# Row broadcasts in a three-block kernel: from a diagonal and a product to transposes of a repeated column

## The chip, the cores and the metric

The kernel runs on one core of one Trainium2 chip. The metric is the device time of an execution in microseconds; of each kernel several runs are taken and their median is compared. Profiles are of one execution each, with times from the start of its span.

## The reference

Three residual blocks follow each other, on 1024 tokens of 1024 features, all in float32. Cut to what the change touches:

```python
def rmsnorm(x, g):                      # before every block part, on branches, at the end
    return x * rsqrt(mean(x * x, -1) + EPS) * g

def first_block(x, mem, ...):
    h = rmsnorm(x, norm_g)
    x_m, o_m, z_m, q_d, k_d, v_d, z_d, q_c, z_c = split(h @ w_in)
    y_m = mlstm(...)                    # below, 4 heads, chunks of 128 tokens
    y_d = rmsnorm(diff_attention(q_d, k_d, v_d), dnorm_g) * silu(z_d)   # per head
    y_c = attention over rmsnorm(mem, mem_norm_g) * silu(z_c)
    return rmsnorm(x + concat(y_m, y_d, y_c) @ w_out, final_g)

def mlstm step(C, n, m; q, k, v, i, b):     # one chunk of one head, b = cumsum(log f)
    m_t = maximum(b + m, max_s(d)),  d[t, s] = b[t] - b[s] + i[s]  for s <= t
    s_qk = (q k^T) * exp(d - m_t)           # the row m_t over all keys
    h = (s_qk v + exp(b + m - m_t) C q) / maximum(|den|, exp(-m_t))
```

Block 2 is chunked attention and spatial gating, then a gated feed-forward; block 3 is a gated recurrence and a long convolution, each with an RMS norm of its branch, then a squared-ReLU feed-forward. Each begins and ends with RMS norms like the one above.

## The kernel before

Activations lie with features on the partitions and tokens on the free axis, in two halves of 512 tokens. Large products split both operands into a high and a low part (`split`, L151 and L152) and take three matmuls each (`mm3`, L142 to L144), in units of eight times three matmuls of 512 columns. Weights come through `wraw` and are split by L76 (ScalarE) and L77 (VectorE).

A norm over features is a sum over partitions, so its scale comes out by tokens. `norm_gen` makes it for one half: the squares are summed in `acc` (at the seams between blocks by GpSimd, L183), `sums_to_cols` (L191) turns the sums into columns `ps[:, t]` with one token per partition, L285 and `rsqrt` (L167 to L172, eleven small VectorE instructions) give the scales `nr`, and `bcast_cols` must spread them: every partition needs the row of all 512 scales. It multiplies the identity by the scales into `diag` (L198, VectorE), and a product of an all-ones matrix with `diag` (L202) puts the row on every partition of a PSUM tile `tp`. ScalarE copies it to `rbc` (L298), and eight `nt` tiles (L301) with their splits are the normed tokens that the next products read.

`bcast_cols` is called 30 times: in `norm_gen` for the five norms at the seams and the two spilled ones (14), once for the memory (256 columns), eight times for the heads of the differential attention (`diff_end`), four times for the branches of block 3 (`branch_norm`), and three times at the end (`final_gen`, pieces of 512, 256 and 256 tokens). A seam does the last products of a block by halves, so the norm of the first half runs beside the products of the second.

The mLSTM is `mlstm_gen` and, per head, `mlstm_head`. Its maxima are rows of a tile `nM`: 32 partitions (head, chunk), 128 tokens each. For four chunks at a time the head computes scores (L808, `k` and `q`) into one half of a PSUM tile and the row of `nM` that belongs to the chunk, on all partitions, into the other (L809: a repeated column of the identity with 32 partitions, times `nM`). VectorE, ScalarE and VectorE make `dm` of both (L813 to L816), and products follow with L825, L840 and L850. Four heads with two such groups make eight blocks.

The work is written as generators: the large products yield after every twelve matmuls, and at each yield every side generator (norms, heads) goes one step. A scheduler then sets the order on each engine by priorities and by its own estimate of when operands are ready; ends of products go ahead by `PRIO_E`. Each engine takes its instructions in that order. Small temporaries, `diag` and `nt` among them, share the pool `half` with four buffers; `tp` has two.

Of the kernel before, what the change touches and what calls it, by code (L numbers as in the profile page):

```python
# [8 lines left out]
F32 = mybir.dt.float32  # L9
# [11 lines left out]
# the ends of products go ahead of other instructions on their engines, by so many  # L21
PRIO_E = 300
# units of products between the end of a half and its norm, by the norm's gain
LEAD = dict(norm_g=1, norm_mix_2=3, norm_ffn_2=3, norm_mix_g_3=3, norm_mlp_g_3=3)
LEAD_F = 2
FINAL = (0, 512), (512, 256), (768, 256)   # pieces of the tokens in the last products
FF_GROUPS = (2, 4, 4, 4, 4, 4)
# units of weights that go ahead on the first half of the tokens after a norm
LAG = 3
LAG_3 = 4  # L30
# products into block 3: values and gates of the long convolution, inputs and gates of the recurrence
SEQ_3 = ["v0 g0 x0 v1 g1 x1 v2", "g2 x2 v3 g3 x3 l0 l1 l2 l3"]   # the convolution of a pair after each
UNITS_3 = [(c[0], int(c[1])) for q in SEQ_3 for c in q.split()]

# ---------------------------------------------------------------- column vectors, one column per 128 features
# [16 lines left out]
class Weights:  # L52
    """The packed weight units in the order of their use: loaded ahead, split into high and low parts."""
# [35 lines left out]
class Kern:  # L89
# [8 lines left out]
    # ------------------------------------------------------------ driver  # L98
# [15 lines left out]
    # ------------------------------------------------------------ tiles  # L114
# [21 lines left out]
    # ------------------------------------------------------------ pieces  # L136
    def mm3(self, ps, w, woff, wn, x, xoff, xn, first, last):
        """ps += w^T x with both operands in two parts; w: [128, 2, .], x: [128, 2, .]."""
# [7 lines left out]
    def split(self, dst, off, n, src, scale=None):  # L146
        """dst[:, 0/1, off:off+n] = high and low part of src (* scale)."""
# [9 lines left out]
    def split2(self, dst, off, n, src):  # L157
        """the same into two tiles"""
        hi, lo = (d[:, off:off + n] for d in dst)
        self.nc.scalar.copy(hi, src)  # L160
        self.nc.vector.tensor_sub(lo, src, hi.bitcast(F32))

    def rsqrt(self, y, v, n, parts=128):
        """y = 1/sqrt(v) for small [parts, n] tiles."""
# [9 lines left out]
    def square_sum(self, acc, src, first, scale=1.0, eng=None):  # L174
        """acc (+)= (src * scale)^2"""
# [12 lines left out]
    def sums_to_cols(self, ps, off, acc, n):  # L188
        """ps[:, off+t] = sum over partitions of acc[:, 128 t + partition]"""
# [4 lines left out]
    def bcast_cols(self, cols, n):  # L194
        """[128, n*128] psum: every partition holds the row whose columns are cols[:, :n]"""
        nc = self.nc
        d = self.half_tmp("diag")
        nc.vector.tensor_tensor(d[:, :n * 128].rearrange("p (t c) -> p t c", t=n),  # L198
# [1752 lines left out]
```

## Time and profile before

| | |
|---|---|
| runs, us | 3480.6, 3486.04, 3488.21 |
| median, us | 3486.04 |
| span of the profiled execution, us | 3484.2 |
| TensorE busy | 3385.5 us, 97% |
| VectorE busy | 1750.7 us, 50% |
| ScalarE busy | 1054.5 us, 30% |
| GpSimd busy | 248.0 us, 7% |
| chain that ended last | TensorE 85%, VectorE 8%, issue 4%, ScalarE 2%, DMA 1% |

A busy TensorE is not one at its peak: matmuls overlap, and a record runs from its start to its modelled end. How long an instruction holds the engine is read from start to start in the view of instructions in order of time. Idle time before an instruction counts only where the engine is the one that sets the end.

### The profile page before, as it was taken

To read this page: it belongs to the slowest core of one execution; us is meant where nothing else is said; L and a number is where in the kernel's file an instruction comes from. 1 tells how busy PE (TensorE), PEld (TensorE's weight loads), DVE (VectorE), ACT (ScalarE), POOL (GpSimd) and SP (SyncE) were. 2 spreads that over 40 slices of the span, in tenths; PEclk is the share of its full clock that TensorE was granted. 3 is DMA by queue.
4 is the path that set the end of the run, shared out by engine and by line. 5 is a ranking of instruction groups with operands and counts; after the bars stand their busy time and mean duration, and the time that the engine had idled before them with its cause. 6 is when DMAs were issued, how large, how long until landed. Compare 5 with 4: busy or idle time off the path is not lost.

```text
span 3484.2 us, 41001 instructions
## 1 busy us (share of the span) xinstructions
PE 3385.5 (97%) x16424; PEld 2750.6 (79%) x16424; DVE 1750.7 (50%) x3329; ACT 1054.5 (30%) x1853; POOL 248.0 (7%) x239
## 2 busy tenths in 40 slices
PE   7999999999999999999999999999999999999998
PEld 6787877777778888887788888877877788888887
DVE  7455556664755561546432333354569833333334
ACT  4222244433444532213111111144443421111112
POOL 0000000002100000102000000040211200000002
PEclk9999999999999999999999999999999999999999
DMA  5123211312111243421111111122111111111111
GB/s 182 62 95 117 79 61 43 110 67 85 61 45 45 73 162 142 148 85 44 61 49 49 49 49 49 49 85 62 45 49 73 37 55 49 49 49 49 49 49 55
DMA packets 98383, 245.06 MB, mean 70 GB/s; under 512 B 12944, under 2 KB 31504, under 8 KB 98192
## 3 DMA queue, kind: packets, MB, share of 16 engines
q1 hardware_dynamic: 84816, 199.92, 16.6%
q0 software_dynamic: 11360, 39.80, 3.3%
q8 instruction: 129, 2.11, 0.2%
q10 hardware_dynamic: 2016, 2.72, 0.2%
q14 instruction: 62, 0.51, 0.0%
HBM read 196.20 MB, written 46.20 MB: 70 GB/s over the span
## 4 chain that ended last, share of the span: by engine, by line
PE 85%; DVE 8%; issue 4%; ACT 2%; DMA 1%; POOL 0%; POOLq 0%; SPq 0%; DVEq 0%; ACTq 0%
PE mm L142 24%; PE mm L143 24%; PE mm L144 24%; PE mm L1614 1%; DVE sp L152 1%; PE tp L202 1%; DVE wsplit L77 1%; DVE nt L301 1%; PE tp L142 1%; PE tp L143 1%; PE sc L934 1%; PE sc L1213 1%; PE tp L1232 1%; PE tp L191 1%; PE tp L144 1%
## 5 line engine op out<-in xcount | busy, mean ns | idle before, releaser
L142 PE MATMUL mm<-sp,wsplit 128*128 128x512 f32 x3424 | 1366.7, 400 | 9.4 <-DVE g L1024 3.9
L143 PE MATMUL mm<-sp,wsplit 128*128 128x512 f32 x3424 | 1349.1, 394 | 12.0 <-DVE sp L152 11.1
L144 PE MATMUL mm<-sp,wsplit 128*128 128x512 f32 x3424 | 1350.3, 395 | 0.0
L142 PEld LDWEIGHTS mm<-sp,wsplit 128*128 128x128 f32 x3424 | 648.1, 189 | 155.4 <-issue 9.8
L143 PEld LDWEIGHTS mm<-sp,wsplit 128*128 128x128 f32 x3424 | 649.4, 190 | 144.0 <-DVE sp L152 14.2
L144 PEld LDWEIGHTS mm<-sp,wsplit 128*128 128x128 f32 x3424 | 648.5, 189 | 137.5 <-issue 3.5
L76 ACT CAST wsplit<-wraw 128x1024 fp32r<-128x1024 f32 x264 | 276.7, 1048 | 675.4 <-PE mm L144 629.6
L77 DVE TENSOR_TENSOR wsplit<-wraw,wsplit 128x1024 fp32r<-128x1024 f32 x264 | 325.7, 1234 | 177.2 <-ACT wsplit L76 175.7
L183 POOL TENSOR_TENSOR acc<-acc,sqt 128x512 f32<-128x512 f32 (+1 forms) x105 | 139.7, 1342 | 1525.7 <-ACT sqt L182 1437.1
L142 PE MATMUL mm<-hid,wsplit 128*128 128x512 f32 (+1 forms) x544 | 207.3, 381 | 0.0
L143 PE MATMUL mm<-hid,wsplit 128*128 128x512 f32 (+1 forms) x544 | 207.1, 381 | 0.0
L144 PE MATMUL mm<-hid,wsplit 128*128 128x512 f32 (+1 forms) x544 | 206.3, 379 | 0.0
L1480 DVE TENSOR_TENSOR u<-u,mm 128x512 f32<-128x512 f32 x144 | 98.9, 687 | 185.3 <-PE mm L144 185.2
L1117 DVE SCALAR_TENSOR_TENSOR u<-mm,u 128x512 f32<-128x512 f32 x128 | 88.0, 690 | 170.0 <-PE mm L144 170.0
L1498 DVE TENSOR_TENSOR hd<-hd 128x512 f32<-128x512 f32 x64 | 44.3, 692 | 190.5 <-ACT hd L1497 190.5
L142 PEld LDWEIGHTS mm<-hid,wsplit 128*128 128x128 f32 x544 | 102.2, 188 | 21.5 <-issue 0.2
L143 PEld LDWEIGHTS mm<-hid,wsplit 128*128 128x128 f32 x544 | 102.5, 188 | 20.9 <-issue 0.2
L144 PEld LDWEIGHTS mm<-hid,wsplit 128*128 128x128 f32 x544 | 102.2, 188 | 20.2
L384 DVE SCALAR_TENSOR_TENSOR silu<-silu,mm 128x512 f32<-128x512 f32 x44 | 30.2, 687 | 165.9 <-ACT silu L383 165.9
L1497 ACT ACTIVATE hd<-mm 128x512 f32<-128x512 f32 x64 | 38.2, 598 | 219.1 <-PE mm L144 219.1
L1163 DVE TENSOR_TENSOR silu<-silu,mm 128x512 f32<-128x512 f32 x44 | 30.2, 687 | 126.8 <-PE mm L144 126.8
L383 ACT ACTIVATE silu<-mm 128x512 f32<-128x512 f32 x44 | 26.3, 598 | 184.1 <-PE mm L144 184.1
(511 smaller groups left out, 3792.7 us busy)
## 6 DMA issues: line engine op xcount, KB each, us to landing
wraw<-W SPq DMA_DIRECT2D x264, 512.0 KB, 3.2
x_d<-u SPq DMA_DIRECT2D x32, 256.0 KB, 2.0
t_d<-gl SPq DMA_DIRECT2D x32, 256.0 KB, 2.0
u<-x_d POOLq DMA_DIRECT2D x16, 512.0 KB, 6.3
gl<-t_d POOLq DMA_DIRECT2D x32, 256.0 KB, 3.1
x<-xT SPq DMA_DIRECT2D x16, 256.0 KB, 5.4
u<-xT POOLq DMA_DIRECT2D x8, 512.0 KB, 6.0
bias<-bias POOLq DMA_DIRECT2D x4, 640.0 KB, 4.2
```

What stands on the lines that cost most here:

```text
L76: K.nc.scalar.copy(s[:, 0, :], r)
L77: K.nc.vector.tensor_sub(s[:, 1, :], r, s[:, 0, :].bitcast(F32))
L142: t.matmul(ps, wh, xh, start=first, stop=False)
L143: t.matmul(ps, wh, xl, start=False, stop=False)
L144: t.matmul(ps, wl, xh, start=False, stop=last)
L152: nc.vector.tensor_sub(lo, src, hi.bitcast(F32))
L183: eng.tensor_add(acc, acc, t[:, :acc.shape[-1]])
L191: self.nc.tensor.matmul(ps[:, off + t:off + t + 1], acc[:, t * 128:(t + 1) * 128], self.ones[:, 0:1], start=True, stop=True)
L1117: nc.vector.scalar_tensor_tensor(uu(m, h), ps, 0.5, uu(m, h), op0=OP.mult, op1=OP.add)
L1480: nc.vector.tensor_add(uu(m, h), uu(m, h), ps)
L1497: nc.scalar.activation(t, ps, AF.Relu)
L1498: nc.vector.tensor_mul(t, t, t)
```

## The change

`bcast_cols` no longer builds a diagonal. For each of its columns it calls a new function `row_of`, which transposes the column, read 128 times over, with the identity: four transposes of 128 columns (two in the narrow calls) take the place of one VectorE instruction and one product. The mLSTM uses the same function: `nM` is transposed once in the preparation into 32 more columns of `mcols`, and each row product L809 becomes a transpose of one such column. Comments are dropped as well; line numbers after L196 move by one or two.

```diff
     def bcast_cols(self, cols, n):
-        nc = self.nc
-        d = self.half_tmp("diag")
-        nc.vector.tensor_tensor(d[:, :n * 128].rearrange("p (t c) -> p t c", t=n),
-                                self.ident[:, None, :].to_broadcast([128, n, 128]),
-                                cols[:, :n, None].to_broadcast([128, n, 128]), op=OP.mult)
         ps = self.tp()
-        nc.tensor.matmul(ps[:, :n * 128], self.ones, d[:, :n * 128], start=True, stop=True)
+        for t in range(n):
+            self.row_of(ps[:, t * 128:t * 128 + 128], cols[:, t:t + 1])
         return ps
...
+    def row_of(self, out, col):
+        self.nc.tensor.transpose(out, col.to_broadcast([128, 128]), self.ident)
...
         nc.tensor.matmul(ps[:, 128:160], self.ones[:32, :], d[:32, :32], start=True, stop=True)
-        cols = self.small([128, 160], F32, "mcols", 1)
-        nc.vector.tensor_copy(cols, ps[:, :160])
+        nc.tensor.transpose(ps[:, 160:192], nM, self.ident[:32, :32])
+        cols = self.small([128, 192], F32, "mcols", 1)
+        nc.vector.tensor_copy(cols, ps[:, :192])
...
                 nc.tensor.matmul(ps[:, c * 128:c * 128 + 128], k[:, s], q[:, s], start=True, stop=True)
-                nc.tensor.matmul(ps[:, 512 + c * 128:640 + c * 128],
-                                 self.ident[:32, r0 + c:r0 + c + 1].to_broadcast([32, 128]), nM, start=True, stop=True)
+                self.row_of(ps[:, 512 + c * 128:640 + c * 128], cols[:, 160 + r0 + c:161 + r0 + c])
```

The order on the engines follows. A row is line, operation, output tile, its operands (the moving one first) and size; the new transposes carry L203. On TensorE, the end of the first mLSTM block before (scores, row, then the first products of a branch):

```order
L808 MATMUL sc<-mq,mk 128x128
L809 MATMUL sc<-rw,ident 128x128
L142 MATMUL mm<-sp,wsplit 128x512
L143 MATMUL mm<-sp,wsplit 128x512
L144 MATMUL mm<-sp,wsplit 128x512
```

and now, where the scores have moved to L809:

```order
L809 MATMUL sc<-mq,mk 128x128
L203 MATMUL sc<-ident,mcols 128x128
L142 MATMUL mm<-sp,wsplit 128x512
L143 MATMUL mm<-sp,wsplit 128x512
L144 MATMUL mm<-sp,wsplit 128x512
```

The order is the same; the row product is now a transpose. On TensorE, at the norm of the second half of the tokens ahead of block 1 (`nr` are its scales), the difference:

```order
-L142 MATMUL mm<-sp,wsplit 128x512
-L143 MATMUL mm<-sp,wsplit 128x512
-L144 MATMUL mm<-sp,wsplit 128x512
-L142 MATMUL mm<-sp,wsplit 128x512
-L202 MATMUL tp<-diag,ones 128x512
+L203 MATMUL tp<-ident,nr 128x128 x4
+L142 MATMUL mm<-sp,wsplit 128x512
+L143 MATMUL mm<-sp,wsplit 128x512
+L144 MATMUL mm<-sp,wsplit 128x512
+L142 MATMUL mm<-sp,wsplit 128x512
```

Four products that stood ahead of the broadcast stand behind it. The same is found at nearly every norm: nine products at both halves of the seams ahead of blocks 2 and 3 but one (three there), seven at the first halves of the two other seams, two to six elsewhere. On VectorE, at the first seam, first half, behind the last step of the reciprocal square root before:

```order
L172 SCALAR_TENSOR_TENSOR nr<-rsq_t,nr 128x8
L77 TENSOR_TENSOR wsplit<-wraw,wsplit 128x1024
L198 TENSOR_TENSOR diag<-ident,nr 128x512
L557 TENSOR_TENSOR u_5896<-u_5896,mm 128x512
L301 SCALAR_TENSOR_TENSOR nt<-u_5888,ngg,rbc 128x512
```

and now:

```order
L172 SCALAR_TENSOR_TENSOR nr<-rsq_t,nr 128x8
L77 TENSOR_TENSOR wsplit<-wraw,wsplit 128x1024
L301 SCALAR_TENSOR_TENSOR nt<-u_5894,ngg,rbc 128x512
L557 TENSOR_TENSOR u_5902<-u_5902,mm 128x512
L301 SCALAR_TENSOR_TENSOR nt<-u_5896,ngg,rbc 128x512
```

The diagonal is gone from between the scales and the first normed tile (the numbers behind `u` are names of the eight tiles of the residual, and are counted otherwise in the two programs).

## Rows read from the trace of the kernel before

**Rows 1.** The page: busy time and share by engine; granted clock in 40 slices.

```profile
PE 3385.5 (97%) x16424; PEld 2750.6 (79%) x16424; DVE 1750.7 (50%) x3329; ACT 1054.5 (30%) x1853; POOL 248.0 (7%) x239
...
PEclk9999999999999999999999999999999999999999
```

**Rows 2.** Groups by line and shape, TensorE: busy us, mean ns | idle before.

```profile
L1232 PE MATMUL tp<-ident,p 128*128 128x128 f32 x240 | 39.1, 277 | 2.6 <-DVE p L1223 0.8 <-DVE pt L152 0.7 <-DVE sp L152 0.7
...
L202 PE MATMUL tp<-diag,ones 128*128 128x512 f32 x54 | 34.7, 732 | 18.6 <-DVE diag L198 18.2
...
L202 PE MATMUL tp<-diag,ones 128*128 128x256 f32 x6 | 3.1, 619 | 10.1 <-DVE diag L198 10.1
```

**Rows 3.** TensorE in order of time, dense broadcast: start us, us, line.

```profile
2773.15 1.02 PE L202 MATMUL tp<-diag,ones 128*128 128x512 f32 x2
...
2774.24 0.40 PE L142 MATMUL mm<-sp,wsplit 128*128 128x512 f32 x1
2774.47 0.39 PE L143 MATMUL mm<-sp,wsplit 128*128 128x512 f32 x1
```

**Rows 4.** The same view: four transposes among products.

```profile
614.15 0.60 PE L542 MATMUL tp<-ident,vt 128*128 128x128 f32 x4
...
614.81 0.39 PE L143 MATMUL mm<-sp,wsplit 128*128 128x512 f32 x1
```

**Rows 5.** The same view: broadcasts at half clock, idle time in brackets.

```profile
832.20 3.75 PE L202 MATMUL tp<-diag,ones 128*128 128x512 f32 x4 [2.72 <-DVE diag L198]
...
2619.70 2.08 PE L202 MATMUL tp<-diag,ones 128*128 128x512 f32 x2 [3.61 <-DVE diag L198]
```

**Rows 6.** Views of lines L809 and L808: count, ns min/median/max, first and last start.

```profile
L809 PEld LDWEIGHTS sc<-rw,ident x64: 180/182/184, 179.1 to 360.8; 32*128 32x128 f32 x64
...
L808 PEld LDWEIGHTS sc<-mq,mk x64: 186/188/192, 178.7 to 360.4; 128*128 128x128 f32 x64
```

**Rows 7.** TensorE in order of time: the first mLSTM block, start and end.

```profile
178.80 0.38 PE L808 MATMUL sc<-mq,mk 128*128 128x128 f32 x2
...
182.02 0.76 PE L142 MATMUL mm<-sp,wsplit 128*128 128x512 f32 x1
```

**Rows 8.** The same view: sixteen records on 128 partitions.

```profile
174.13 1.95 PE L789 MATMUL sc<-mw,xm 128*128 128x128 f32 x16
175.84 0.36 PE L142 MATMUL mm<-wsplit,sp 128*128 128x256 f32 x1
```

**Rows 9.** Busy time by stretch, sum of seven stretches from 76 to 420 us.

```profile
sum 344.00, PE 343.04 PEld 272.97 DVE 183.32 ACT 89.11 POOL 3.75; mean PE 49.01 PEld 39.00 DVE 26.19 ACT 12.73 POOL 0.54
```

**Rows 10.** View of line L198: count, ns min/median/max.

```profile
L198 DVE TENSOR_TENSOR diag<-ident,nr x17: 426/691/1769, 38.0 to 3476.1; 128x512 f32<-128x512 f32 x15, 128x256 f32<-128x256 f32 x2
```

**Rows 11.** Chain that ended last, first seam: start us, us, what.

```profile
872.92 1.76 DVE diag L198
```

**Rows 12.** TensorE in order of time, first seam.

```profile
892.68 0.80 PE L143 MATMUL mm<-sp,wsplit 128*128 128x512 f32 x1 [2.71 <-DVE sp L152]
```

**Rows 13.** Chain that ended last, at the end of the program.

```profile
3476.14 0.44 DVE diag L198
...
3476.63 1.24 PE tp L202 x2
```

**Rows 14.** Busy time of L809 by stretch: us, PE (x), PEld (x), clock, DMA.

```profile
178.67:182.08 3.41, 1.92 (x8) 1.17 (x8) 1.00 0.30 92
...
342.51:345.92 3.41, 1.91 (x8) 1.14 (x8) 1.00 0.20 77
```

**Rows 15.** By stretch: us, PE, PEld, DVE, ACT, POOL busy (x), clock, DMA.

```profile
182.08:185.49 3.41, 3.41 (x9) 2.71 (x9) 1.82 (x5) 0.63 (x1) 0.00 (x0) 0.50 0.74 254
...
345.92:349.33 3.41, 3.41 (x9) 2.67 (x9) 1.40 (x4) 0.63 (x1) 0.00 (x0) 0.50 0.47 159
898.88:1612.20 713.32, 704.99 (x3695) 580.84 (x3693) 369.98 (x818) 256.53 (x547) 51.45 (x72) 1.00 0.27 92
```

More of the change, by code (lines that the diff above doesn't have):

```diff
@@ L740, in mlstm_gen @@
         nc.tensor.matmul(ps[:, 128:160], self.ones[:32, :], d[:32, :32], start=True, stop=True)
-        cols = self.small([128, 160], F32, "mcols", 1)
-        nc.vector.tensor_copy(cols, ps[:, :160])
+        nc.tensor.transpose(ps[:, 160:192], nM, self.ident[:32, :32])
+        cols = self.small([128, 192], F32, "mcols", 1)
+        nc.vector.tensor_copy(cols, ps[:, :192])
         yield
-        self.mctx = (xcv, xm, cols, nM)
+        self.mctx = (xcv, xm, cols)
         for h in range(4):
@@ L763, in mlstm_head @@
         nc, v, A = self.nc, self.v, self.A
-        xcv, xm, cols, nM = self.mctx
+        xcv, xm, cols = self.mctx
         ks = 128 ** -0.5
```

## Prediction

> **What bounds the kernel now.** Read the page first: TensorE is busy 97% of the span, VectorE 50%, and the granted TensorE clock is near full in every slice [rows 1]. So TensorE's own work is the bound, and VectorE matters only where TensorE stands and waits for it. Three questions follow: how long does TensorE hold for the work that the change replaces, how long does it wait for the diagonals, and at which clock does it run there. The grouped view answers the second: before the products of the row broadcasts TensorE sat idle 18.2 + 10.1 = 28.3 us for the diagonal of L198 [rows 2]. That is the whole wait, of which the diagonal is only the last link; the sums, the scaling and the reciprocal square root stand before it and stay.
>
> **Term A: the broadcast's product, 30 calls.** 27 calls have 512 columns and 3 have 256; the 54 and 6 records of [rows 2] are two passes for each. In a dense stretch the pair starts at 2773.15 and the second product behind it at 2774.24, 1.09 us later, with one ordinary product (0.23 us from start to start) in between: 0.86 us of TensorE [rows 3]. The new form is four transposes of 128 columns. Four transposes of a value tile start at 614.15 and the second product behind them at 614.81: 0.66 - 0.23 = 0.43 us [rows 4]. So a wide call saves 0.43 us and a narrow one half of it: 27 x 0.43 + 3 x 0.215 = 12.3 us. Five calls ran at half clock, where both forms cost double: the two that start at 832.20 take 3.75 us together, the last of the five, at 2619.70, takes 2.08 [rows 5]. Each is worth another 0.43 us: 2 us.
>
> The stationary operand of the new transposes is one column read 128 times. The row products of the mLSTM have such an operand already, a repeated column of the identity, and its load takes 182 ns, no more than the 188 ns of a full tile [rows 6]. So I charge nothing for the repetition.
>
> **Term B: the rows of the mLSTM, 8 blocks.** Each block has four score products (L808) and four row products (L809, 32 partitions) in turn, two records each. The first holds TensorE from 178.80 to 182.02, 3.22 us [rows 7]; the seven others are built alike. Sixteen records of the same kind as L808's, all on 128 partitions (L789), start at 174.13, and the next product at 175.84 [rows 8]: 1.71 us, with what the next one loses about 1.8, or 0.11 each. In the block a record holds TensorE for 0.2 us; the alternation between 128 and 32 partitions is the only difference that the rows show. The change removes it: the row comes from a transpose over 128 partitions. Eight score records at 0.11 and four transposes at 0.11 make 1.33 us. Saved: 1.89 x 8 = 15.1 us. In the stretches from 76 to 420 us, which hold the mLSTM, TensorE is busy for 343 of 344 us and VectorE for 183 [rows 9], so this is gained in full: the products of the output gates and branches fill the time. The dm chain behind the block keeps the same twelve products ahead of L840 as its cover. If a record of the new block holds 0.2 us like one of the old, the block is 12 x 0.2 = 2.4 us or a little more and B is about 6. I take 15.1, as the rows of L789 are the nearer ones; 6 stays as the lower end. The one new transpose in the preparation (0.11 us) and the copy that is 32 columns wider are counted as nothing, since dense products surround them.
>
> **Term C: waits.** The diagonal takes 0.69 us in the median and 0.43 at 256 columns, but up to 1.77 [rows 10]; 1.75 or more are those at the first and third seam, while GpSimd adds squares. Taking it away shortens a wait by no more than its time and a handover of 0.06. TensorE stood idle before 16 of the 30 calls: three long diagonals at 1.81, six at 0.75, three narrow ones at 0.49 and four waits that were shorter than the diagonal (0.86 together) give 12.2 us at most. Where the norm holds up TensorE to its end, all of that counts: at the first seam the chain is diagonal (872.92, 1.76 us), product, scaled tokens [rows 11], and TensorE waits again, 2.71 us, for the last split of that chain at 892.68 [rows 12]. So it is at the third seam (two waits), at the second and fourth, at 832, in the norm of the memory and at the very end, where 0.44 us of diagonal and a product of 1.24 us follow each other [rows 13]. These make 3 x 1.8 + 3 x 0.75 + 2 x 0.5 = 8.7, and the shorter last product some 0.5 more than A has counted: 9 us.
>
> Against that stands the order: the scheduler now puts the transposes up to nine products earlier. TensorE takes its work in order, so products that used to run ahead of the broadcast and cover the reciprocal square root now stand behind it. Where the norm is not waited for later (second halves of the seams, branch norms, the last pieces, the differential heads), some 50 small and large products are moved, by 0.23 us for a large one [rows 3] about 11 us; the diagonals there and the slack that the old order had give some 7 back. So I take 4 us off: C = 9 - 4 = 5. Its ends are -7 (the moved products cost more than their diagonals save, the seams give nothing) and 12. The second broadcast at the seams that spill a norm needs no wait of its own any more, as its scales are ready with the first; that is within these ends.
>
> **Term D: the clock.** Three stretches of the mLSTM ran at half clock, 182.08 to 185.49 the first and 345.92 to 349.33 the last [rows 15]. What TensorE did before each was such a block: the 3.41 us ahead of it hold all eight row records of one [rows 14]. The other five blocks were followed by none. A block of 1.33 us leaves dense products in the rest of such a stretch, so I expect the three to go: 3.41 us at half clock loses 1.7 us, three times, 5.1 us. Ends 0 and 10, if a low stretch at a seam goes as well.
>
> **Off the path:** 30 diagonals, some 20 us of VectorE's time, and the buffers of the `half` pool that they held. VectorE is not the bound; at the seams this is inside C. VectorE gets no new work but the 32 columns.
>
> **Sum.** A 12.3 + 2, B 15.1, C 5, D 5.1: 39.5 us off the profiled span of 3484.2 gives 3444.7. The median of the runs, 3486.04, lies 1.9 us above that span, so 3447 us.
>
> **Rivals.**
> *The block keeps its cost* (B at 6, D at 0): 12.3 + 2 + 6 + 5 = 25 us, 3461. For it: L808's records, on 128 partitions themselves, hold 0.2 us in the block too [rows 7], so the turn from one kind of product to another may be what costs. Against: products behind transposes start without such a delay [rows 4]. Chance 0.14.
> *The order takes the waits back* (C at -7): 27.5 us, 3459. For it: the order shows the shift at nearly every norm. Against: the starved seams are limited by the chain and not by where the broadcast stands. Chance 0.15.
> *More goes than that* (C at 12, D at 10): 51.4 us, 3435. Chance 0.05.
> *The clock falls behind transposes, slower than before.* If a group of transposes is idleness to the clock, each of the 30 calls and 8 blocks is followed by a stretch like that of [rows 15], 1.7 us lost: 38 x 1.7 = 65 us, against 34 us gained without D. That gives 3517; it decides from about 20 of the 38 places on. The trace speaks against it: 240 transposes of L1232 [rows 2] lie in the attention of block 2, and from 898.88 to 1612.20 the clock was 1.00 [rows 15]. Chance 0.03. The Trainium skill says just this of the clock (TensorE: Matmul & The Clock Gate, Part 4: PE-mode transpose): a transpose does not count as work for the clock, and the full rate does not engage on it. By that rule the time would be this rival's; the trace does not bear it out for groups of two to four transposes among products.
> *It doesn't do what it says*: the repeated column loads slowly. At four times the 0.11 us the 38 groups would take 1.3 us more each, 49 us, and the gain of 39.5 would turn to a loss of 10, 3496. Against: the load of 182 ns [rows 6]. Chance 0.03.
> The forecast keeps 0.60.
>
> **Range and chances.** About 0.2% (7 us) is what a measurement of this kernel can tell from no change. The forecast's own spread is some 9 us, from the places where half-clock stretches happen to fall. Down to 3434 the range takes in the case of more, up to 3465 the two cases of less; the slower rivals and the tails, about 0.16, stay outside. Faster: the forecast, both cases of less and that of more, 0.94, less a little for tails: 0.92. Same 0.03, slower 0.05.
>
> **What would show it.** Right: four transposes hold TensorE 0.43 us in a dense stretch; the mLSTM block lasts 1.3 us, and no half clock follows it; the idle time before the broadcasts stays near 28 us, now against the reciprocal square root, while the waits for the splits at the seams shrink by 1 to 2 us. Wrong: a block of over 2 us; idle time before the transposes well over 30 us with the waits at the seams unchanged; half-clock stretches in dense parts that had none; weights (L77) that come later because VectorE's order has changed.

## The result, and the profile after

The changed kernel took 3446.97 us in the median (3442.71 to 3449.89), the kernel before 3483.32 (3477.88 to 3488.21): a ratio of 0.9894, with a 95% interval of 0.988 to 0.9908. Faster by 36 us. The forecast was 3447, which was 39 us below the 3486.04 that the kernel before had then. Two repeats beside the experiments below gave 3450.03 and 3450.85 us, ratios 0.9911 and 0.9914, or 30 to 32 us. The time lies in the forecast's range; of the four terms, the mLSTM's held, and the others need the account at the end.

The page of the profiled execution (span 3441.0 us): busy time by engine, and the chain that ended last by engine.

```profile
PE 3343.3 (97%) x16447; PEld 2730.7 (79%) x16447; DVE 1732.3 (50%) x3299; ACT 1054.0 (31%) x1853; POOL 249.8 (7%) x239
...
PE 82%; DVE 8%; issue 7%; ACT 2%; DMA 1%; POOL 0%; POOLq 0%; DVEq 0%; SPq 0%; ACTq 0%
```

Against [rows 1], TensorE is busy for 42 us less and the span is 43 us shorter. What is left, TensorE's idle time, was 98.7 us and is 97.7: the change took work off TensorE (and time at half clock, which counts as busy), and in sum it took off hardly any waiting. That is the first thing to read here, since term C had 5 us for waits.

TensorE in order of time, a broadcast in a dense stretch, beside [rows 3]: start us, us, line, shapes.

```profile
2730.90 0.60 PE L203 MATMUL tp<-ident,nr 128*128 128x128 f32 x4
2731.25 0.48 PE L142 MATMUL mm<-sp,wsplit 128*128 128x512 f32 x1
2731.57 0.39 PE L143 MATMUL mm<-sp,wsplit 128*128 128x512 f32 x1
```

From 2730.90 to the second product behind, less one product of 0.23: 0.44 us, where 0.86 stood. And the first mLSTM block, beside [rows 7]:

```profile
175.88 0.39 PE L809 MATMUL sc<-mq,mk 128*128 128x128 f32 x2
176.11 0.27 PE L203 MATMUL sc<-ident,mcols 128*128 128x128 f32 x1
...
177.10 0.27 PE L203 MATMUL sc<-ident,mcols 128*128 128x128 f32 x1
177.13 0.48 PE L142 MATMUL mm<-sp,wsplit 128*128 128x512 f32 x1
```

Twelve records, 0.11 us from one start to the next, 1.25 us to the next product and about 1.33 with what that product loses; the block of before held 3.22. All eight are alike (1.24 or 1.25 us). The loads of the repeated column (count, ns min/median/max, first and last start) cost no more than those of full tiles in [rows 6]:

```profile
L203 PEld LDWEIGHTS tp<-ident,nr x64: 132/136/227, 36.5 to 3433.9; 128*128 128x128 f32 x64
L203 PEld LDWEIGHTS sc<-ident,mcols x32: 137/139/139, 176.0 to 337.3; 128*128 128x128 f32 x32
```

The part of the program with the blocks lies between the first transpose of the gates (L700) and the last transpose of the heads (L878). Those two lines, of the kernel before and then of the changed one:

```profile
L700 PE MATMUL tp<-ident,gt x1: 270/270/270, 145.6 to 145.6; 128*32 128x128 f32 x1
L878 PE MATMUL tp<-ident,ht x32: 270/327/330, 215.0 to 380.1; 128*128 128x128 f32 x32
```

```profile
L700 PE MATMUL tp<-ident,gt x1: 270/270/270, 142.6 to 142.6; 128*32 128x128 f32 x1
L878 PE MATMUL tp<-ident,ht x32: 270/327/332, 206.5 to 356.4; 128*128 128x128 f32 x32
```

234.5 us became 213.8. By stretch (length, then busy time and count by engine, granted clock, DMA), the changed kernel has full clock there (granted 1.00, the level of 2.4 GHz), and over most of what follows; the second line is one of its stretches at half clock (0.50, 1.2 GHz):

```profile
76.00:398.00 322.00, 321.05 (x1757) 260.11 (x1756) 181.15 (x511) 88.98 (x144) 3.76 (x7) 1.00 0.28 94
807.56:817.80 10.24, 7.30 (x20) 5.37 (x21) 5.89 (x12) 3.60 (x6) 1.73 (x3) 0.50 0.22 64
872.41:2319.66 1447.25, 1429.62 (x6906) 1179.31 (x6906) 642.15 (x1186) 407.31 (x756) 89.67 (x102) 1.00 0.21 73
```

None of the three half-clock stretches of [rows 15] is left. The Trainium skill (TensorE: Matmul & The Clock Gate, Part 4: PE-mode transpose) holds that a transpose does not count for the clock; here the 32 transposes of the blocks stand in the first stretch and the clock stays at 1.00, so groups of this size among products do not bring it down. Whether a transpose alone would keep it up, no run here shows.

Last, the idle time of TensorE just before the broadcasts (busy us, mean ns | idle before, by what ended it):

```profile
L203 PE MATMUL tp<-ident,nr 128*128 128x128 f32 x64 | 10.2, 280 | 7.7 <-DVE nr L172 7.6
```

Together with 5.9 us before the two transposes of the memory's norm, 2.5 before the heads' and 2.5 before the branch norms' it is 18.6 us, where [rows 2] had 28.7 (28.3 of it for the diagonal). It fell by 10 us, and yet the sum of all idle time stayed nearly the same: the waiting went elsewhere. The forecast had said the opposite, that these 28 us would stay and other waits shrink.

### The profile page after: what moved, and what is told of

It is laid out like the page before. It is cut to its first block, busy times and chain, and to the rows that moved or that the text cites. A ratio compares the mean times of both kernels' runs of the same rounds, so it can differ in the third digit from the quotient of the medians.

```text
span 3441.0 us, 41019 instructions
## 1 busy us (share of the span) xinstructions
PE 3343.3 (97%) x16447; PEld 2730.7 (79%) x16447; DVE 1732.3 (50%) x3299; ACT 1054.0 (31%) x1853; POOL 249.8 (7%) x239
## 4 chain that ended last, share of the span: by engine, by line
PE 82%; DVE 8%; issue 7%; ACT 2%; DMA 1%; POOL 0%; POOLq 0%; DVEq 0%; SPq 0%; ACTq 0%
PE mm L142 24%; PE mm L143 24%; PE mm L144 23%; DVE sp L152 1%; PE mm L1614 1%; DVE nt L301 1%; DVE wsplit L77 1%; PE sc L1213 1%; PE tp L1232 1%; PE tp L142 1%; PE tp L143 1%; PE tp L191 1%; PE tp L144 1%; PE sc L934 1%; DVE wsplit L1596 0%
## 5 line engine op out<-in xcount | busy, mean ns | idle before, releaser
L142 PE MATMUL mm<-sp,wsplit 128*128 128x512 f32 x3424 | 1362.0, 398 | 15.7 <-DVE u L1117 4.1
```

Of the source, the lines that this page charges most:

```text
L142: t.matmul(ps, wh, xh, start=first, stop=False)
```

## Experiments

Each theory is told with its run. The first question is which half of the change gives what; the second, what the alternation of 128 and 32 partitions and what the diagonal itself had cost; the third, what half clock is worth. A fourth came up on the way.

**The changed kernel again.** No edit.

> The changed kernel once more, five rounds, so that the others of this call have it beside them. If what differs between its executions is the clock alone, its times and granted clocks go together: a mean clock lower by 0.001 is about 6.9 us more at half clock and so at most 3.4 us more time. Expected 3442 to 3450 us with clocks of 0.993 to 0.991.

3450.03 us (3448.99 to 3452.46), ratio 0.9911 [0.9897, 0.9924].

> The changed kernel as it is, as the control for the three kernels beside it: 3447 to 3451 us where the kernel before takes 3482, ratio .990 to .991. Between its profiled executions the mean granted clock should again decide: .991 goes with a span of about 3448 us, .993 with about 3441.

3450.85 us (3448.97 to 3454.06), ratio 0.9914 [0.99, 0.9927]. The profiled spans were 3447.8 and 3448.8, that of the first profile 3441.0. Part of the difference is half clock in the differential attention, between the first transpose of its values and the last of its probabilities: 6.8 us in the first profile, 17.1 and 27.3 in these, 3.4 before. The stage is 2.9 and 6.6 us longer than in the first profile. In the first repeat the start of the program, up to the gates, took another 3.0 us more, and in both the second seam 1.6. Two such stretches of the third profile, by length, busy time and count of TensorE, its loads, VectorE, ScalarE and GpSimd, granted clock, DMA:

```profile
671.64:681.88 10.24, 10.12 (x27) 6.25 (x27) 7.06 (x17) 5.02 (x13) 0.13 (x1) 0.50 0.44 176
750.15:760.39 10.24, 10.24 (x21) 5.99 (x21) 4.89 (x9) 2.15 (x5) 0.00 (x0) 0.50 0.01 2
```

**The broadcasts alone.** The mLSTM is as before (the diff is cut to its row products):

```diff
-                self.row_of(ps[:, 512 + c * 128:640 + c * 128], cols[:, 160 + r0 + c:161 + r0 + c])
+                nc.tensor.matmul(ps[:, 512 + c * 128:640 + c * 128],
+                                 self.ident[:32, r0 + c:r0 + c + 1].to_broadcast([32, 128]), nM, start=True, stop=True)
```

> Only the 30 broadcasts are changed; the mLSTM rows are made as before, by L809-like products on 32 partitions. By the prediction's terms A and C: 12 + 2 + 5 = 19 us faster than before, about 3464. If the idle time is only moved (C = 0), 12 to 14 us, about 3470. If the broadcasts bring only clock, and TensorE's saved work is lost at the seams, under 9 us. In both, the mLSTM blocks still take 3.2 us each and two to four of them are followed by half clock.

3467.39 us (3466.68 to 3472.34), ratio 0.9963 [0.995, 0.9975]: 14.3 us gained. The forecast for this half was 14.3 of work (A) and 5 of waits (C). Half clock behind blocks of the old form is there again, though only twice in this execution, and the part with the blocks took 233.0 us instead of 234.5: the third stretch had cost about half its length.

```profile
236.44:239.86 3.42, 3.42 (x9) 2.65 (x9) 1.70 (x5) 0.63 (x1) 0.00 (x0) 0.50 0.49 153
359.32:362.74 3.42, 3.42 (x10) 2.64 (x9) 1.35 (x4) 0.63 (x1) 0.00 (x0) 0.50 0.00 0
```

**The mLSTM alone.** The broadcasts are as before (the diff is cut):

```diff
-        for t in range(n):
-            self.row_of(ps[:, t * 128:t * 128 + 128], cols[:, t:t + 1])
+        d = self.half_tmp("diag")
+        nc.vector.tensor_tensor(d[:, :n * 128].rearrange("p (t c) -> p t c", t=n),
+                                self.ident[:, None, :].to_broadcast([128, n, 128]),
+                                cols[:, :n, None].to_broadcast([128, n, 128]), op=OP.mult)
+        nc.tensor.matmul(ps[:, :n * 128], self.ones, d[:, :n * 128], start=True, stop=True)
```

> The changed mLSTM alone (row_of for the scores, the norms' broadcasts by diagonal and ones as before). Theory (the two halves of the change do not touch each other): the kernel with the broadcasts alone was 14.3 us faster than before, the whole change 31.7, so this one gains 17 us, or 20.7 by the stage from the mLSTM's gates to its end (234.5 to 213.8 us); no half clock in that stage. Rival (the halves share waits on VectorE, so the gain of one depends on the other): less than 14 us or more than 24 us.

3463.71 us (3460.48 to 3466.82), ratio 0.9948 [0.9936, 0.9961]: 17.5 us gained. With the other half 31.8, and the whole gained 30.4 and 31.7 in the two repeats: the halves add up, as the theory had it. Inside, the mLSTM part took 213.8 us here as in the whole change, 20.7 less than before. That the run gained only 17.5 has a likely place a stage later: the differential attention had 10.2 us at half clock, where the profiles of the kernels with the old blocks had 3.4 to 6.8, and from the third head's sums to the fourth's it took 89.8 us instead of 86.6. These are single executions, so it is a reading and no proof.

**The row as an ordinary product.** The same operands and the same place, but no transpose: two records for each row, 128 partitions.

```diff
-        self.nc.tensor.transpose(out, col.to_broadcast([128, 128]), self.ident)
+        self.nc.tensor.matmul(out, col.to_broadcast([128, 128]), self.ident, start=True, stop=True)
```

> As the changed kernel, but row_of is an ordinary product of the same two operands (repeated column, identity) and no transpose: two passes in place of one, still on 128 partitions, still without a diagonal. A wide broadcast then holds TensorE 8 x 0.11 = 0.88 us again, 12 us in all, and an mLSTM block 16 x 0.11 = 1.8 us, 3.6 us in all: 3460 to 3465. That is if the old block was long because it alternated between 128 and 32 partitions. If it was long because products and row products alternated at all, the blocks stay near 3 us and the half clock behind them comes back: 3475 to 3482.

3458.79 us (3457.11 to 3461.31), ratio 0.9938 [0.9924, 0.9951], 8.8 us above the changed kernel beside it. That is less than the 15.6 us which the expectation had for the additional records. Its profile ran 42.0 us at half clock, that of the changed kernel beside it 61.5; half of the difference is 9.8 us and would explain what is missing, but no run shows that the two belong together. TensorE in order of time, start and end of its first block:

```profile
177.82 0.39 PE L809 MATMUL sc<-mq,mk 128*128 128x128 f32 x2
178.04 0.39 PE L203 MATMUL sc<-ident,mcols 128*128 128x128 f32 x2
...
179.38 0.39 PE L203 MATMUL sc<-ident,mcols 128*128 128x128 f32 x2
179.53 0.47 PE L142 MATMUL mm<-sp,wsplit 128*128 128x512 f32 x1
```

Sixteen records, as many as in [rows 7], in 1.71 us instead of 3.22, and the part took 217.2 us with no half clock. So 1.5 of the 1.9 us a block had nothing to do with transposing: two kinds of product in turn cost nothing, products on 128 and on 32 partitions in turn cost nearly twice their time. This settles the rival in which the block keeps its cost. The four records fewer are the rest.

This run changed the operands together with the partitions, so look at where the time went in the old block. Its loads of stationary operands, kernel before, in order of time:

```profile
178.68 0.31 PEld L808 LDWEIGHTS sc<-mq,mk 128*128 128x128 f32 x2
179.11 0.29 PEld L809 LDWEIGHTS sc<-rw,ident 32*128 32x128 f32 x2
179.52 0.30 PEld L808 LDWEIGHTS sc<-mq,mk 128*128 128x128 f32 x2
```

Two loads on the same number of partitions overlap and start 0.11 us apart. At a change of the number the next load starts only 0.12 us after the last has ended, about 0.3 us from start to start. It is so at all 64 changes in the eight blocks, in both directions, and 8 x 0.19 us is the 1.5 us of a block. With the ordinary product, loads of two kinds on 128 partitions start 0.11 us apart throughout. Elsewhere in the kernel before, from products on 48 partitions (L1399) to products on 16 (L1400), the loads are 0.21 us apart at all twelve changes and 0.11 within a pair.

**The repeated columns written out by VectorE.** All else is as changed; the transposes read a tile of 512 columns that VectorE has to fill first, so the chain has its old length and the products their new one.

```diff
+        d = self.half_tmp("diag")
+        self.nc.vector.tensor_tensor(d[:, :n * 128].rearrange("p (t c) -> p t c", t=n),
+                                     self.ones[:, None, :].to_broadcast([128, n, 128]),
+                                     cols[:, :n, None].to_broadcast([128, n, 128]), op=OP.mult)
         for t in range(n):
-            self.row_of(ps[:, t * 128:t * 128 + 128], cols[:, t:t + 1])
+            self.nc.tensor.transpose(ps[:, t * 128:t * 128 + 128], d[:, t * 128:t * 128 + 128], self.ident)
```

> As the changed kernel, but VectorE writes the repeated columns of a broadcast into a tile of 512 columns (one instruction of 0.69 us, in the place and of the size of the old diagonal), and the transposes read that tile. TensorE's work is that of the changed kernel, VectorE's chain that of before. Term C as predicted (the diagonal was worth time on the chains of the seams): 5 us slower than the changed kernel, up to 9. If VectorE's part was worth nothing, since the idle time of TensorE is as long without it: within 2 us of the changed kernel.

3454.94 us (3451.13 to 3455.62), ratio 0.9921 [0.9908, 0.9935], 4.9 us above the changed kernel by the medians, with intervals that overlap.

**The diagonal built, and read by no one.** VectorE has its old work, behind the transposes; the chain to the transposes is the new one.

```diff
         for t in range(n):
             self.row_of(ps[:, t * 128:t * 128 + 128], cols[:, t:t + 1])
+        d = self.half_tmp("diag")
+        self.nc.vector.tensor_tensor(d[:, :n * 128].rearrange("p (t c) -> p t c", t=n),
+                                     self.ident[:, None, :].to_broadcast([128, n, 128]),
+                                     cols[:, :n, None].to_broadcast([128, n, 128]), op=OP.mult)
```

> The changed kernel, and VectorE still builds each diagonal, behind the transposes in the order of the program, where nothing reads it. Theory (what the diagonal's removal is worth is its place in the chain from norm to transposes): within 2 us of the control, and the idle time of TensorE before the broadcasts stays at 18 to 20 us. Rival (what counts is VectorE's time, some 30 operations of about .7 us to 1.8 us at the seams where it is the last to finish): 3 to 6 us slower than the control, with the waits for sp from VectorE longer by a microsecond at each seam.

3453.77 us (3451.0 to 3456.57), ratio 0.9919 [0.9905, 0.9932]: 2.9 us above its control, with intervals that overlap too. The times can't tell these two apart, but the traces can, at the first seam. Sums of the squares of the one half and of the other start it and end it; here are both rows of the changed kernel (first profile), of the written-out columns, and of the unread diagonal:

```profile
841.09 1.84 PE L191 MATMUL tp<-ones,acc 128*128 128x1 f32 x16
874.78 1.84 PE L191 MATMUL tp<-ones,acc 128*128 128x1 f32 x16
```

```profile
844.76 1.84 PE L191 MATMUL tp<-ones,acc 128*128 128x1 f32 x16
878.11 1.84 PE L191 MATMUL tp<-ones,acc 128*128 128x1 f32 x16
```

```profile
847.99 1.84 PE L191 MATMUL tp<-ones,acc 128*128 128x1 f32 x16
883.70 1.84 PE L191 MATMUL tp<-ones,acc 128*128 128x1 f32 x16
```

33.7, 33.3 and 35.7 us; the kernel before took 35.8. At the third seam it is 33.8, 33.4, 35.0 and 36.3. What tells them apart is the order of the instructions. Before, 26 products stood between the sums and the broadcast there, and the written-out kernel keeps these 26, with a VectorE operation still between the norm and its broadcast. The changed kernel and the one with the unread diagonal have 17. So the pairs can be compared: with the new order, taking the diagonal off VectorE is worth 2.0 and 1.2 us at these seams; with the diagonal there, the new order costs 2.4 and 1.6. The two cancel. What the seams did gain, 2 to 2.5 us, is there with the diagonal in the chain as well. That fits the shorter products and a shorter time at half clock (10.2 us before, 6.8 in the written-out kernel, 3.4 in the two others at the first seam). Part of it is the execution: the kernel with the mLSTM alone, which has the old broadcasts, took 34.7 and 35.8 us. In the changed kernel the wait for the last split is no shorter than the 2.71 us of [rows 12] (idle time in brackets):

```profile
868.51 0.50 PE L143 MATMUL mm<-sp,wsplit 128*128 128x512 f32 x1 [2.97 <-DVE sp L152]
```

At the first branch norm of block 3 it is otherwise. From the sums of its first half to those of its second, the kernels with the old order took 13.5 to 15.9 us (before 15.9, mLSTM alone 13.5, written-out columns 14.9). All three profiles of the changed kernel, the broadcasts alone and the unread diagonal took 10.8. With half of the time at half clock taken off, 12.4 to 13.0 stand against 10.8. So here the shorter chain with its earlier broadcast gained some 2 us, of which the piece behind it lost 0.4 to 0.7 again. It is also the place where the written-out kernel falls behind the changed one, by 4.1 us; at the two seams it is not behind.

**Products that fill the idle time.** At 808, 868, 2320, 2581 and 2698 us TensorE stood idle for 1.9 to 3 us just before a half-clock stretch or in it. Products whose results count for nothing were put there. They were meant to take 1.1 us at each place; in the trace they take 1.15 us at 868 and 2320 (five records), but 2.2 us at the three others, where ten products are twenty records. The diff is cut to the function and the tile:

```diff
+    def fill(self, ps, n, col=None):
+
+        w = self.ones if col is None else col.to_broadcast([128, 128])
+        for _ in range(n):
+            self.nc.tensor.matmul(ps[:, :128], w, self.ident, start=True, stop=True)
...
+                if fill and i == 0 and k == 4:
+                    for _ in range(fill):
+                        self.nc.tensor.matmul(ps[:32, :N], self.zw, src(0, h)[:, 0, :N], start=False, stop=False)
...
+        self.zw = c.tile([128, 32], F32R, name="zw")
+        nc.scalar.activation(self.zw, self.ones[:, :32], AF.Copy, scale=0.0)
```

> The changed kernel with five stretches of products that count for nothing (1.1 us each), put where the trace shows TensorE idle for 1.9 to 3 us just before or in a half-clock stretch (near 808, 868, 2320, 2581 and 2698 us): products of a column or of ones into a PSUM tile that is overwritten, products with a zero operand in the first unit after two seams. Theory (the clock falls because of the idle time): these half-clock stretches are gone or shorter, 10 us less at half clock in the profiled execution, the time 3 to 8 us below the control. Rival (the fall follows something else, or the idle is mended too little): half clock as in the control, and the time 0 to 4 us above it, by the products that run into the chain.

3438.04 us (3433.32 to 3441.18), ratio 0.9873 [0.9859, 0.9886]: 12.8 us below the changed kernel beside it, more than twice the middle of what the theory had. Half clock was gone at four of the five places. At the branch norms the fills did harm: before a broadcast at 2604 TensorE now waited 4.6 us where it had waited 0.5. But the largest difference stood where no fill was: from the sums of the last seam to those of the first final piece, dense products at full clock, 679.1 us had become 672.5.

**The tile without the fills.** The kernel with the fills also had a new tile of zeros, 128 bytes on each partition, ahead of all later tiles. This kernel has the tile and no fills:

```diff
         nc.vector.memset(self.ones, 1.0)
+        self.zw = c.tile([128, 32], F32R, name="zw")
+        nc.scalar.activation(self.zw, self.ones[:, :32], AF.Copy, scale=0.0)
```

> The changed kernel with only the tile of zeros that the kernel with the fills had (128 bytes on each partition, ahead of all later tiles), and no fills. In the last products between 2740 and 3400 us the profiled start-to-start of products from hid was 226.7 ns in the kernel with the fills and 231.1 ns in every other one, 6.6 us in that stretch, where no fill stands. Theory (the place of the tiles in SBUF, moved by 128 bytes): 226.7 ns here too, and 6 to 7 us below the control, 3444 us. Rival (it came with the fills, by the higher clock or the changed order): 231.1 ns, and 3449 to 3452 us.

3439.2 us (3437.11 to 3445.53), ratio 0.9878 [0.9863, 0.9894]; the interval lies below those of the two repeats of the changed kernel (from 0.9897 and 0.99), but overlaps that of its first set (0.988 to 0.9908). The same stretch of last products in the changed kernel (third profile) and with the tile: length, TensorE's busy time and records, its loads, the other engines, clock.

```profile
2790.00:3400.00 610.00, 610.00 (x2665) 500.50 (x2664) 217.56 (x277) 120.02 (x167) 2.58 (x2) 1.00 0.13 46
```

```profile
2790.00:3400.00 610.00, 610.00 (x2692) 505.08 (x2692) 219.59 (x280) 121.05 (x168) 5.14 (x4) 1.00 0.13 46
```

Both are busy all the time at full clock, and one gets 27 products more through, 6 us. From one start to the next, products that read the hidden tiles (`hid`) take 231.1 ns in the mean in the kernel before, the changed kernel and all the others told of so far but the one with the fills, and 226.7 ns in that one and here. In the old place the distances run from 224 to 241 ns; with the tile they are 226 or 227 throughout. The groups by line and shape say it too (busy us, mean ns), changed kernel and then the tile:

```profile
L143 PE MATMUL mm<-hid,wsplit 128*128 128x512 f32 x480 | 189.1, 394 | 0.0
```

```profile
L143 PE MATMUL mm<-hid,wsplit 128*128 128x512 f32 x480 | 186.7, 389 | 0.0
```

Over 1,432 such distances that is 6.4 us. By the medians the tile is 11.7 us below the changed kernel, where the theory had 6 to 7. Some 3.7 us more came at the start of the program, up to the first products of normed tokens at 53 us, but at the gates, near 143 us, 1.0 of it was left (6.8 us at half clock had come at 71). They also came with the next tile, and whether the place or the new ScalarE instruction brings them was not separated; what makes up the rest stays open.

**Twice the tile.**

```diff
-        self.zw = c.tile([128, 32], F32R, name="zw")
-        nc.scalar.activation(self.zw, self.ones[:, :32], AF.Copy, scale=0.0)
+        self.zw = c.tile([128, 64], F32R, name="zw")
+        nc.scalar.activation(self.zw, self.ones[:, :64], AF.Copy, scale=0.0)
```

> The same with 256 bytes. If it is the place of the tiles that counts: either 226.7 ns again (any shift away from the old place mends it) or 231.1 ns (the old place is one of a regular pattern of 256 bytes, and only odd steps of 128 bytes mend it); the time 3444 or 3450 us accordingly.

The products of `hid` are back at 231.1 ns:

```profile
L143 PE MATMUL mm<-hid,wsplit 128*128 128x512 f32 x480 | 189.2, 394 | 0.0
```

Time 3450.74 us, ratio 0.9901 [0.9885, 0.9917], with a wide spread: two runs at 3439.43 and 3441.79 (mean granted clock 0.993 and 0.992), three from 3450.74 to 3451.99 (0.989 and 0.990). The median says little here; the trace is the answer.

**The tile in the kernel before.** The same edit to the kernel before.

> The kernel before with the tile of 128 bytes. Theory (place of the tiles, which has nothing to do with the change): start-to-start of products from hid 226.7 ns instead of 231.1, and 6 to 7 us below the kernel before, 3475 us. Rival: no difference.

3474.4 us (3468.66 to 3480.98, eleven runs), ratio 0.9983 [0.9974, 0.9992]: 6.5 us faster by the medians, and `hid` at 226.7 ns. So the place of the tiles had cost both kernels' products of `hid` the same 4.5 ns each; it has nothing to do with the change.

**The fills without those at the branch norms.**

```diff
-        self.nb = getattr(self, "nb", 0) + 1
-        bps = self.bcast_cols(rr[:, 4:8], 4, 10 if self.nb == 1 else 0, rr[:, :1])
+        bps = self.bcast_cols(rr[:, 4:8], 4)
```

> The kernel with the fills without the ones at the branch norm near 2581 us, where the time from the sums of the one half to those of the other had grown by 2.7 us and the stage before by 3.0 us. Theory (those fills ran into the chain, the others mend the clock): 3434 to 3437 us, 1 to 4 us below the kernel with all the fills and 8 to 10 us below the kernel with the tile of zeros alone. Rival (all of the gain of the fills was the place of the tiles): no more than 3 us below the kernel with the tile alone.

3437.11 us (3434.72 to 3441.61), ratio 0.9876 [0.9862, 0.989]: 2.1 us below the kernel with the tile alone, inside its interval. The theory's 8 to 10 us fell; the rival, that the gain was the place of the tiles, holds for most of it. The clock did what it was meant to do at three of the four places; at 2321 us a stretch of 3.4 us at half clock came all the same. The places near 811 and 870 us, first in the changed kernel (third profile), then here:

```profile
818.41:825.24 6.83, 5.72 (x13) 4.09 (x14) 3.68 (x6) 3.60 (x6) 2.09 (x3) 0.50 0.37 105
876.44:879.85 3.41, 3.41 (x10) 2.70 (x9) 3.38 (x4) 1.22 (x2) 3.22 (x2) 0.50 0.46 156
```

```profile
811.00:824.00 13.00, 10.37 (x58) 8.24 (x58) 7.89 (x21) 4.52 (x8) 3.73 (x5) 1.00 0.31 93
869.00:876.00 7.00, 3.79 (x15) 2.48 (x15) 6.91 (x8) 2.55 (x4) 3.23 (x2) 1.00 0.39 115
```

But a half-clock stretch costs only about half its length (1.6 us for 3.4 in the part with the blocks, above), and where the stretch lies in front of a wait, a faster TensorE only waits longer: against the kernel with the tile alone, the piece from the last transpose of the probabilities to the next sums fell from 41.1 to 39.4 us, but at the first seam 33.7 grew to 34.2. Other stretches came up elsewhere. This is the fastest kernel by its median, though the tile alone is not told apart from it.

## Why the prediction was right, and where it was not

**Term B held.** 15.1 us were worked out from the sixteen records of [rows 8] against the block of [rows 7]; with the 5.1 us of the three half-clock stretches the part should fall by 20.2 and fell by 20.7. With half of the time at half clock taken off, the part took 229.4 us before and 229.5 in the kernel with the broadcasts alone, and 213.8 now: B measured alone is 15.6 to 15.7. The choice between the ends (6 or 15.1) was made for the nearer row and by the alternation of partitions. The ordinary product in the transposes' place and the loads of the old block show the alternation to be the cause.

**Term A held for one call, and is not shown for all.** 0.43 us by [rows 4], 0.42 measured. In the differential attention, eight calls worth 3.4 us, the stage went from 324.1 to 324.7 us in the first profile and to 327.6 and 331.3 in the repeats. With half the time at half clock taken off, it did fall, from 322.4 to between 317.7 and 321.3. So work went and the clock took it back there; how much of A's 14.3 us reached the end is not known.

**Term C is the step that failed, in its places and, by the traces, in its size.** It said 9 us gained where the chain bounds the seams, less 4 lost to the moved order, and that the idle time before the broadcasts would stay while the waits for splits shrink. Measured: the idle time before the broadcasts fell by 10 us, the wait for the split stayed (2.71 us, 2.97 now), TensorE's idle time as a whole changed by 1 us, and the broadcasts alone gained 14.3 us, no more than A by itself. The mechanism was on the list with both signs, and both are real: 2.0 and 1.2 us for the diagonal at the first and third seam, 2.4 and 1.6 for the order. The loss was charged in the wrong place: where the norm is not waited for later, the branch norms among them. It also falls on the chain-bound seams, where the products that the transposes were moved past had been covering the reciprocal square root, and there it eats the gain; at the first branch norm there was a gain instead. The size is less certain than the places. By the medians, the written-out columns are 4.9 us above the changed kernel, which is C's 5, and they gain 9.3 us over the mLSTM alone, which is less than A's 14.3. The intervals of these times overlap or nearly do, and the clock differs between the profiles, so the times don't settle how the 14.3 us divide into A and C. The rival in which the order takes the waits back was nearer than its 0.15 at the seams (its C of -7 was too much).

**Term D was right in place and wrong in sum.** The three stretches behind the blocks are gone in every profile with the new blocks. But how much of the span runs at half clock was treated as settled outside the mLSTM, and it is not: without the start and the mLSTM's three, and with the tail, the profile before had 73 us of it, the changed kernel 46 in the first profile, 61 and 70 in the repeats. In the differential attention it was 3.4 and 6.8 us in the profiles with the old blocks and is 6.8 to 27.3 in those with the new ones. One place stands out. TensorE waits 1.73 us at 749 in the third profile, just ahead of the stretch at 750.15, and the same wait is in every profile (1.72 us at 769 before). Half clock follows it in ten of the eleven profiles with the new blocks, 6.8 or 10.2 us of it, and in none of the three with the old ones. So the new blocks seem to bring it, and it can take back as much as D gave; a wait alone doesn't decide it. What does, in one execution and not in another, was not found and stays open.

**So the sum held by luck in its last few microseconds.** The forecast of 3447 is the median of the first set to a few hundredths, but it stood for 39 us off 3486.04, the median of three runs; with a fourth run the kernel before has 3483.32, and the gain is 36 us, or 30 to 32 in the repeats. The forecast gain was 3 to 9 us too large. In the first set's profile 27 us less ran at half clock outside the mLSTM, some 13 us that no term had. With it, A, B and D add up to more than the 43 us between the two spans, so some of that work or half clock had cost nothing. 3450 to 3451, from the repeats, is the better value, and it lies inside the range of 3434 to 3465.

**The slower rivals** fell as the trace of before had them: the 32 transposes of the blocks stand in a stretch at full clock, and the loads of the repeated column take 136 to 139 ns.

## What to carry over

Look first for products that change their number of partitions from one to the next: that alternation, and not the amount of work, was 1.5 of the 1.9 us that a block of the mLSTM lost, and giving the small product a full set of partitions removed it. When a step on another engine falls away, see where the scheduler now puts its reader: if it moves ahead of products that used to cover the same wait, the gain of the shorter chain can be gone, as at the seams; measure each place, for at the branch norm it stayed. Judge a gain of a few microseconds by several executions and their granted clock, and change the place of the tiles once before believing it.

## What the runs showed of the hardware

- Pairs of records on 128 and 32 partitions in turn: about 0.2 us a record; the same number on 128 partitions, products of two kinds in turn: 0.107 us. The time is lost at the change: the next load of a stationary operand starts 0.12 us after the last has ended, where otherwise the two overlap.
- A transpose of 128 float32 columns holds TensorE for 0.11 us, an ordinary float32 product of the same shape for two such records. A stationary operand that repeats one column is loaded in 136 to 139 ns in the median in a transpose, as a full tile is (139 ns, L878), and in 192 ns in the ordinary product of the mLSTM's rows.
- 128 bytes more ahead of the tiles made neighbouring products of the hidden tiles (1,432 distances) 226.7 ns apart instead of 231.1; 256 bytes left them at 231.1. The Trainium skill (SBUF — State Buffer, SBUF: two separate sides) says that TensorE's port waits for no one and that DMA and engines can't contend. No run here speaks against the ports, but the place of an operand did matter, by 2% of dense products. Which operand it is, and what in its place, stays open.
- Half clock came where TensorE had stood idle for about 2 or 3 us (1.98 us at 816, 2.97 at 876, in the third profile), not at each such place in each execution. It also came without such a wait: behind the old blocks, and at 623.9 us in the third profile, where no wait above 0.12 us stands in the 11 us before. The products that count for nothing kept the clock full at 811, 870 and 2698 in the two kernels that had them there; at 2321 they did so in one of the two.
